# Two heads of a pair by turns in both halves of TensorE's columns, and one exponential and mask for both, in the parallel mixers of a two-block network

## The chip, the core and the metric

The kernel runs on one core of a Trainium2 chip. The metric is the device time of one execution in microseconds; three runs of the kernel before gave 2126.7, 2129.07 and 2130.88 us. The engines are named as in the profile: PE (TensorE, matmuls), DVE (VectorE), ACT (ScalarE), POOL (GpSimd) and SP (which issues the loads).

## The reference

Two different transformer-like blocks follow each other on a sequence of 256 tokens with 1024 features, each of two layers. The change lies in the second block. It puts 16 meta tokens ahead (272 tokens), and each of its layers has a feed-forward part, three mixers side by side and another feed-forward part. The mixers share one input projection and one output projection:

```python
proj = h @ w_in[l]
(z, xbc, dt_raw, fq, fk, fv, f_raw, cq, ckv, k_rope) = jnp.split(proj, IN_SPLITS, axis=-1)
mix = jnp.concatenate([y_ssd, y_fox, y_mla], axis=-1) @ w_out[l]

# fox (4 heads of 64, forget gates c) and mla (4 heads of 96 and 64): causal attention
p = jax.nn.softmax(jnp.where(causal, s, -jnp.inf), axis=-1)
out = jnp.einsum('bhqk,bkhd->bqhd', p, v)

# ssd (8 heads of 64, 2 groups): a state-space mixer, in its quadratic form
seg = jnp.exp(jnp.where(causal, a_cum[..., :, None] - a_cum[..., None, :], -jnp.inf))
cb = jnp.einsum('bclhn,bcshn->bhcls', Cm, Bm)
y_diag = jnp.einsum('bhcls,bcshp->bclhp', cb * seg, xdt)
```

## The kernel before

Features lie on partitions and tokens along the columns. Weight matrices are split in two parts (`wh`, `wl`) on ACT (L100) and DVE (L101), and a projection to 128 features is 24 matmuls over the full array (`pj`, L128 in the mixers, L730 to L732 for the output projection).

`Second.mixer` runs once for each of the two layers. It is a set of generators, each of which yields after a small step: the input projection, `gates`, `latents`, `heads`, `states`, two `attend` for each kind of attention and `ssd`. `run_spread` takes the next step from the generator that is furthest behind its share of the stage. The framework then gives every engine a fixed order of its own, so that PE takes its instructions in that order and one that waits holds back all behind it. Heads go in pairs: with 64 features a head, heads `2c` and `2c + 1` fill the lower and the upper half of the 128 partitions of one PSUM bank (`yp` for attention, `sy` for the decay, one bank each).

In `attend`, a unit is one head `hh` of the pair and one block `i` of queries: `i = 0` the 16 meta tokens (both heads at once), `i = 1` and `i = 2` the blocks of 128. Three steps follow each other, each one turn of the loop behind the other: `score` (PE L558 into `S`, then DVE and ACT: mask, L566 exponential), `turn` (DVE L575, PE transposes L580 into `pt`, copies to `apt` by DVE L581 and ACT L584) and `apply` (PE L597 into `yp`, L592 for `i = 0`). Applying block `i` takes one matmul with the 16 rows of the meta tokens and `i` matmuls with 128 rows, each with 64 stationary columns (the head's `v`) and 128 moving ones.

In `ssd`, each head's cumulated decay is broadcast by two matmuls (L404, L405 into `bc`). For each of the three blocks of keys (`STT`, 128, 128 and 16 rows) DVE subtracts (L661), ACT takes the exponential (L662), DVE multiplies by the masked product `cbm` (L649), and PE multiplies by `xdt` into the head's half of `sy` (L650), with 64 stationary and 272, 144 or 16 moving columns (256 instead of 272 in the last layer, which computes no meta tokens). `held` lets two further blocks start before a block is finished. L669 and what follows it turn `sy` into the output part `yo`.

All these matmuls are float32, which are two records of the trace each; those of the projections (float32r) and the transposes are one record.

Of the kernel before, what the change touches and what calls it, by code (L numbers as in the profile page):

```python
# [10 lines left out]
F32 = mybir.dt.float32  # L11
F32R = mybir.dt.float32r
AF = mybir.ActivationFunctionType
ALU = mybir.AluOpType
ADD, SUB, MUL, MIN, MAX = ALU.add, ALU.subtract, ALU.mult, ALU.min, ALU.max
# [9 lines left out]
STT = [(0, 128), (128, 128), (256, 16)]  # L25
# [276 lines left out]
class Second:  # L302
# [28 lines left out]
    def mixer(self, l, xs, sp, f0):  # L331

        n, nc, P = self.n, self.n.nc, self.n.P
        T, TQ = T2, T2 - f0
        tc = self.n.tc
        with ExitStack() as es:
            es.enter_context(n.psum(pj=2, pt=1, yp=1, bc=1, S=2, sy=1))
            kp = es.enter_context(tc.tile_pool(name="mk", bufs=1))
            tp = es.enter_context(tc.tile_pool(name="mt", bufs=2))
            win = f"w_in{l}"  # L340
            kt = lambda name, w=T, dt=F32: kp.tile([128, w], dt, name=name)
            tt_ = lambda name, w=T, bufs=1: tp.tile([128, w], F32, name=name, bufs=bufs)
            pj = lambda: n.ps("pj", T)
            mm = nc.tensor.matmul
# [9 lines left out]
            toks = kp.tile([128, 3, 72], F32, name="toks")  # L354
# [151 lines left out]
            cbm = []  # L506
# [27 lines left out]
            def attend(c, q, k, v, fox):  # L534

                yp = n.ps("yp", T)
                units = ([] if f0 else [(0, 0)]) + [(hh, i) for i in (1, 2) for hh in range(2)]
                ckbs, tiles, pts = {}, {}, {}

                def score(hh, i):  # L540
                    h = 2 * c + hh
                    q0, qn = FQT[i]
                    kn = q0 + qn
                    if fox and i == 1:
                        ckbs[hh] = tt_("ckb", bufs=2)
                        nc.scalar.copy(ckbs[hh], bcast(32 + h))
                    S = n.ps("S", T)
                    if i == 0:
                        qn = 64
                        for e in range(2):  # L550
                            o = S[32 * e:32 * e + 32, :kn]
                            if fox:
                                j = 32 + h + e
                                mm(o, n.ident[32:64, j:j + 1].to_broadcast([32, 32]), cum[32:64, :kn], start=True, stop=False)
                                mm(o, cum[32:64, 0:32], self.nid[32:64, j:j + 1].to_broadcast([32, kn]), start=False, stop=False)
                            mm(o, q(h + e)[:, 0:32], k(h + e)[:, :kn], start=not fox, stop=True)
                    else:
                        mm(S[:qn, :kn], q(h)[:, q0:q0 + qn], k(h)[:, :kn], start=True, stop=True)  # L558
                    src = S
                    t = tt_("att", bufs=3)  # L560
                    if fox and i:
                        nc.vector.scalar_tensor_tensor(t[:qn, :kn], ckbs[hh][:qn, :kn], tokq[:qn, i, h:h + 1], S[:qn, :kn], op0=SUB, op1=ADD)
                        src = t
                    mn = tp.tile([128, 2], F32, name="amn", bufs=4)
                    nc.vector.tensor_tensor_reduce(t[:qn, :kn], src[:qn, :kn], self.mask[:qn, i, :kn], 1.0, 3.0e38, op0=ADD, op1=MIN, accum_out=mn[:qn, 0:1])
                    nc.scalar.activation(t[:qn, :kn], t[:qn, :kn], AF.Exp, scale=-1.0, bias=mn[:qn, 0:1], accum_out=mn[:qn, 1:2])  # L566
                    tiles[hh, i] = t, mn

                def turn(hh, i):
                    q0, qn = FQT[i]  # L570
                    kn = q0 + qn
                    qn = qn if i else 64
                    t, mn = tiles.pop((hh, i))
                    nc.vector.reciprocal(mn[:qn, 1:2], mn[:qn, 1:2])
                    nc.vector.tensor_scalar(t[:qn, :kn], t[:qn, :kn], mn[:qn, 1:2], None, op0=MUL)  # L575
                    ps = n.ps("pt")
                    pt = pts[hh, i] = tp.tile([128, 3, 128], F32, name="apt", bufs=2)
                    for j in range(i + 1):
                        k0, kk = FQT[j]
                        nc.tensor.transpose(ps[:kk, j * 128:j * 128 + qn], t[:qn, k0:k0 + kk], n.ident[:qn, :qn])  # L580
                    nc.vector.tensor_copy(pt[:16, 0, :qn], ps[:16, :qn])  # L581
                    if i:
                        w = slice(128, 128 + i * 128)
                        nc.scalar.copy(pt[:, 1:1 + i], ps[:, w].rearrange("p (a b) -> p a b", b=128))  # L584

                def apply(hh, i):
                    h = 2 * c + hh
                    q0, qn = FQT[i]
                    pt = pts.pop((hh, i))
                    if i == 0:  # L590
                        for e in range(2):
                            mm(yp[64 * e:64 * e + 64, 0:16], v[:16, 0, 64 * (h + e):64 * (h + e) + 64], pt[:16, 0, 32 * e:32 * e + 16], start=True, stop=True)  # L592
                        return
                    rows = slice(64 * hh, 64 * hh + 64)
                    for j in range(i + 1):
                        kk = FQT[j][1]
                        mm(yp[rows, q0:q0 + qn], v[:kk, j, 64 * h:64 * h + 64], pt[:kk, j, :qn], start=(j == 0), stop=(j == i))  # L597

                for u in range(len(units) + 2):
                    if u < len(units):  # L600
                        score(*units[u])
                    if 0 <= u - 1 < len(units):
                        turn(*units[u - 1])
                    if u >= 2:
                        apply(*units[u - 2])
                    if u == len(units) + 1:
                        key = (4 if fox else 6) + c
                        ys[key] = n.split(kp, f"yo{key}", yp[:, f0:], TQ)
                    yield
# [5 lines left out]
            xdt = kp.tile([128, 3, 512], F32, name="xdt")  # L615
# [16 lines left out]
            def ssd():  # L632
                for i, (s0, sn) in enumerate(STT):
                    ps = n.ps("pt")
                    for c in range(4):
                        nc.tensor.transpose(ps[:sn, ts(c, 128)], xsn[c][:, s0:s0 + sn], n.ident)
                    nc.vector.tensor_tensor(
                        xdt[:sn, i].rearrange("p (h d) -> p h d", h=8),
                        ps[:sn].rearrange("p (h d) -> p h d", h=8),
                        toks[:sn, i, 64:72].rearrange("p (h o) -> p h o", o=1).to_broadcast([sn, 8, 64]), op=MUL)  # L640
                    yield
                held = []

                def finish():
                    yp, h, i, m = held.pop(0)
                    s0, sn = STT[i]
                    e = max(s0, f0)
                    rows = slice(64 * (h % 2), 64 * (h % 2) + 64)
                    nc.vector.tensor_tensor(m[:sn], m[:sn], cbm[h // 4][i][:sn, e - s0:], op=MUL)  # L649
                    mm(yp[rows, e:], xdt[:sn, i, 64 * h:64 * h + 64], m[:sn], start=(i == 0), stop=(i == 2))  # L650

                for c in range(4):
                    yp = n.ps("sy", T)
                    ysum[c] = kt(f"ys{c}")[:, :TQ]
                    for hh in range(2):
                        h = 2 * c + hh
                        bc = bcast(h)
                        for i, (s0, sn) in enumerate(STT):
                            e = max(s0, f0)
                            m = tt_(f"ssm{i}", T - s0, 2)[:, e - s0:]  # L660
                            nc.vector.tensor_scalar(m[:sn], bc[:sn, e:], toks[:sn, i, h:h + 1], 0.0, op0=SUB, op1=MIN)  # L661
                            nc.scalar.activation(m[:sn], m[:sn], AF.Exp)  # L662
                            held.append((yp, h, i, m))
                            if len(held) > 2:
                                finish()
                            yield
                    while held:
                        finish()
                    nc.vector.scalar_tensor_tensor(ysum[c], xsn[c][:, f0:], P(f"dskip{l}", c), yp[:, f0:], op0=MUL, op1=ADD)  # L669
                    if c % 2:  # L670
                        while 16 + c not in have:
                            yield
                        for e in (c - 1, c):
                            nc.vector.tensor_tensor(ysum[e], ysum[e], zs[e], op=MUL)
                        norms(c // 2)
                    yield
# [1254 lines left out]
```

## Time and profile before

| | |
|---|---|
| median of three runs | 2129.07 us |
| the profiled execution | 2128.95 us |
| its span, first to last instruction | 2127.2 us |
| PE busy | 2061.1 us, 97% of the span |
| DVE busy | 1449.9 us, 68% |
| ACT busy | 1099.4 us, 52% |
| mean DMA rate | 159 GB/s |
| first mixer, first to last 64-column matmul | 1240.2 to 1326.9 us |
| second mixer, the same | 1820.2 to 1898.9 us |

A record's duration of a matmul holds its whole way through the array, and matmuls overlap. So a busy share of 100% doesn't tell how fast PE gets on; the distance from one start to the next does. The rows of a timeline merge records of one line that follow each other; their length is then from the first start to the last end.

### The profile page before, as it was taken

The page shows a single profiled execution, that of the slowest core. Times are in us where ns is not written, and L with a number is a line of the kernel's source. Part 1 is how long each engine was busy: PE and PEld are TensorE (multiplying, and loading weights), DVE is VectorE, ACT ScalarE, POOL GpSimd, SP SyncE. Part 2 cuts the span into 40 slices and gives each one's busy share as a digit, 9 for nine tenths or more (in the row PEclk, how much of TensorE's full clock was granted, in tenths as well). Part 3 has the DMA queues.
Part 4 walks back from the last instruction along what each step waited for, and adds up shares of the span by engine and source line. Part 5 has one row for each costly group of instructions (what it writes and reads, how often), then busy time and mean ns, then how long its engine had stood idle before and what let it go on. Part 6 is the DMA issues. An engine that isn't in the chain of part 4 may idle for free.

```text
span 2127.2 us, 43215 instructions
## 1 busy us (share of the span) xinstructions
PE 2061.1 (97%) x17602; PEld 1910.9 (90%) x17602; DVE 1449.9 (68%) x2959; ACT 1099.4 (52%) x2055; POOL 30.3 (1%) x68
## 2 busy tenths in 40 slices
PE   7999999999899989999999999999999999999998
PEld 6888888999888879999999877899999998778998
DVE  7878776886788867556555776755565457767555
ACT  4544446444745555545454744644454537456453
POOL 0000000000011100000000000000000000000000
PEclk9999999999999999999999999999999999999999
DMA  7533323896434237645554321455455543225553
GB/s 269 169 95 124 96 64 117 329 322 213 147 125 145 92 127 260 197 169 184 188 173 167 131 90 60 128 190 171 161 170 182 164 170 128 90 70 178 189 179 119
DMA packets 102087, 337.30 MB, mean 159 GB/s; under 512 B 11456, under 2 KB 19456, under 8 KB 101888
## 3 DMA queue, kind: packets, MB, share of 16 engines
q1 hardware_dynamic: 101888, 334.54, 47.3%
q8 instruction: 138, 2.26, 0.4%
q14 instruction: 61, 0.50, 0.1%
HBM read 333.45 MB, written 1.05 MB: 157 GB/s over the span
## 4 chain that ended last, share of the span: by engine, by line
PE 86%; DVE 7%; ACT 4%; DMA 2%; issue 1%; POOL 1%; SPq 0%; ACTq 0%; DVEq 0%; POOLq 0%
PE pj L157 17%; PE pj L158 17%; PE pj L160 17%; PE pj L128 8%; PE pj L1067 4%; PE B L918 2%; DVE wl L101 2%; PE yp L597 1%; PE pj L148 1%; ACT wh L100 1%; PE G L1170 1%; PE pj L149 1%; PE B L1371 1%; PE sy L650 1%; PE pj L152 1%
## 5 line engine op out<-in xcount | busy, mean ns | idle before, releaser
L101 DVE TENSOR_TENSOR wl<-wr,wh 128x1024 fp32r<-128x1024 f32 (+2 forms) x557 | 641.1, 1160 | 296.5 <-ACT wh L100 142.3
L100 ACT CAST wh<-wr 128x1024 fp32r<-128x1024 f32 (+2 forms) x557 | 555.7, 1002 | 499.1 <-PE pj L158 207.6
L278 DVE TENSOR_TENSOR hh<-sg,pj 128x256 f32<-128x256 f32 (+1 forms) x132 | 56.5, 428 | 148.9 <-PE pj L160 130.0
L829 DVE SCALAR_TENSOR_TENSOR adacc<-adar,cond,adacc 128x512 f32<-128x512 f32 x140 | 104.2, 744 | 10.4 <-DMA adar<-in_ada_dram 8.9
L187 ACT ACTIVATE q<-r 128x256 f32<-128x256 f32 (+1 forms) x80 | 33.3, 422 | 97.4 <-DVE r L208 79.6
L157 PE MATMUL pj<-s0h,wh 128*128 128x256 f32 (+1 forms) x240 | 68.4, 285 | 0.9 <-ACT wh L100 0.9
L160 PE MATMUL pj<-s6h,wl 128*128 128x256 f32 (+1 forms) x240 | 68.6, 286 | 0.0
L158 PE MATMUL pj<-s5l,wh 128*128 128x256 f32 (+1 forms) x240 | 68.4, 285 | 0.0
L157 PE MATMUL pj<-s6h,wh 128*128 128x256 f32 (+1 forms) x240 | 68.4, 285 | 0.0
L158 PE MATMUL pj<-s7l,wh 128*128 128x256 f32 (+1 forms) x240 | 68.3, 285 | 0.0
L160 PE MATMUL pj<-s1h,wl 128*128 128x256 f32 (+1 forms) x240 | 68.3, 284 | 0.0
L160 PE MATMUL pj<-s5h,wl 128*128 128x256 f32 (+1 forms) x240 | 68.2, 284 | 0.0
L160 PE MATMUL pj<-s7h,wl 128*128 128x256 f32 (+1 forms) x240 | 68.2, 284 | 0.0
L160 PE MATMUL pj<-s0h,wl 128*128 128x256 f32 (+1 forms) x240 | 68.2, 284 | 0.0
L160 PE MATMUL pj<-s4h,wl 128*128 128x256 f32 (+1 forms) x240 | 68.2, 284 | 0.0
L157 PE MATMUL pj<-s4h,wh 128*128 128x256 f32 (+1 forms) x240 | 68.2, 284 | 0.0
L158 PE MATMUL pj<-s1l,wh 128*128 128x256 f32 (+1 forms) x240 | 68.1, 284 | 0.0
L160 PE MATMUL pj<-s2h,wl 128*128 128x256 f32 (+1 forms) x240 | 68.1, 284 | 0.0
L158 PE MATMUL pj<-s3l,wh 128*128 128x256 f32 (+1 forms) x240 | 68.0, 284 | 0.0
L157 PE MATMUL pj<-s7h,wh 128*128 128x256 f32 (+1 forms) x240 | 68.0, 284 | 0.0
L157 PE MATMUL pj<-s1h,wh 128*128 128x256 f32 (+1 forms) x240 | 68.0, 283 | 0.0
L157 PE MATMUL pj<-s5h,wh 128*128 128x256 f32 (+1 forms) x240 | 68.0, 283 | 0.0
(1811 smaller groups left out, 7283.2 us busy)
## 6 DMA issues: line engine op xcount, KB each, us to landing
wr<-in_ffn_in_dram SPq DMA_DIRECT2D x264, 512.0 KB, 3.7
wr<-in_ffn_out_dram SPq DMA_DIRECT2D x96, 512.0 KB, 3.5
adar<-in_ada_dram SPq DMA_DIRECT2D x80, 512.0 KB, 4.7
wr<-in_w_in_dram SPq DMA_DIRECT2D x40, 512.0 KB, 3.5
wr<-in_ffn_out_dram SPq DMA_DIRECT2D x48, 384.0 KB, 3.7
wr<-in_gin_dram SPq DMA_DIRECT2D x32, 512.0 KB, 3.7
ada<-in_ada_dram SPq DMA_DIRECT2D x16, 512.0 KB, 7.2
wr<-in_w_out_dram SPq DMA_DIRECT2D x16, 512.0 KB, 3.4
```

Source lines behind the costliest of these rows:

```text
L100: nc.scalar.copy(h, r)
L101: nc.vector.tensor_tensor(l, r, h.bitcast(F32), op=SUB)
L128: mm(o, a, b[:, t0:], start=(c == 0), stop=(c == 23))
L148: mm(o, wh, xs[k][0], start=(i == 0), stop=False)
L157: mm(o, wh, xs[k][0], start=(i == 0), stop=False)
L158: mm(o, wh, xs[k][1], start=False, stop=False)
L160: mm(o, w(k)[1], xs[k][0], start=False, stop=(i == K - 1))
L187: nc.scalar.activation(q[k], d[k], AF.Square)
L278: nc.vector.tensor_tensor(hh, sg, up, op=MUL)
L829: nc.vector.scalar_tensor_tensor(acc, r[:, ts(k, 512)], c, acc, op0=MUL, op1=ADD)
L918: self.anchor = nc.tensor.matmul(out[r, c], lhsT[r, c], rhs[r, c], start=start, stop=start or b == nblk - 1).ins
L1067: nc.tensor.matmul(ps, a, b, start=(k == 0 and i == 0), stop=(k == 7 and i == 2))
```

## The change

In `attend`, `apply` does nothing for the first head of a pair (but for `i = 0`). With the second head it takes both heads' transposed scores, and for each block of keys issues the matmul of head 1 (upper half of the columns) and then that of head 0 (lower half); `issue_after` keeps these two in that order in PE's queue. `apt` has three buffers instead of two.

In `ssd`, the tiles `ssm` hold both heads side by side, as does the mask by a broadcast. The subtraction stays one for each head. The exponential and the mask are one instruction for both heads, after the second head's subtraction, and the two heads' matmuls follow each other. `held` lets one further block start.

```diff
-                    pt = pts[hh, i] = tp.tile([128, 3, 128], F32, name="apt", bufs=2)
+                    pt = pts[hh, i] = tp.tile([128, 3, 128], F32, name="apt", bufs=3)
...
                 def apply(hh, i):
                     h = 2 * c + hh
                     q0, qn = FQT[i]
-                    pt = pts.pop((hh, i))
                     if i == 0:
+                        pt = pts.pop((hh, i))
...
                         return
-                    rows = slice(64 * hh, 64 * hh + 64)
+                    if hh == 0:
+                        return
+                    pair = [pts.pop((e, i)) for e in range(2)]
                     for j in range(i + 1):
                         kk = FQT[j][1]
-                        mm(yp[rows, q0:q0 + qn], v[:kk, j, 64 * h:64 * h + 64], pt[:kk, j, :qn], start=(j == 0), stop=(j == i))
+                        for e in (1, 0):
+                            g = 2 * c + e
+                            with tc.issue_after(at) if e == 0 else nullcontext():
+                                at = mm(yp[64 * e:64 * e + 64, q0:q0 + qn], v[:kk, j, 64 * g:64 * g + 64], pair[e][:kk, j, :qn], start=(j == 0), stop=(j == i)).ins
...
                 def finish():
-                    yp, h, i, m = held.pop(0)
+                    yp, c, i, m = held.pop(0)
                     s0, sn = STT[i]
                     e = max(s0, f0)
-                    rows = slice(64 * (h % 2), 64 * (h % 2) + 64)
-                    nc.vector.tensor_tensor(m[:sn], m[:sn], cbm[h // 4][i][:sn, e - s0:], op=MUL)
-                    mm(yp[rows, e:], xdt[:sn, i, 64 * h:64 * h + 64], m[:sn], start=(i == 0), stop=(i == 2))
+                    w = T - e
+                    pair = m[:, :2 * w].rearrange("p (h t) -> p h t", h=2)
+                    mask = cbm[c // 2][i][:sn, e - s0:].rearrange("p (o t) -> p o t", o=1).to_broadcast([sn, 2, w])
+                    nc.vector.tensor_tensor(pair[:sn], pair[:sn], mask, op=MUL)
+                    for hh in range(2):
+                        h = 2 * c + hh
+                        mm(yp[64 * hh:64 * hh + 64, e:], xdt[:sn, i, 64 * h:64 * h + 64], pair[:sn, hh], start=(i == 0), stop=(i == 2))
...
+                    ms = [tt_(f"ssm{i}", 2 * (T - s0), 2) for i, (s0, sn) in enumerate(STT)]
                     for hh in range(2):
                         h = 2 * c + hh
                         bc = bcast(h)
                         for i, (s0, sn) in enumerate(STT):
                             e = max(s0, f0)
-                            m = tt_(f"ssm{i}", T - s0, 2)[:, e - s0:]
-                            nc.vector.tensor_scalar(m[:sn], bc[:sn, e:], toks[:sn, i, h:h + 1], 0.0, op0=SUB, op1=MIN)
-                            nc.scalar.activation(m[:sn], m[:sn], AF.Exp)
-                            held.append((yp, h, i, m))
-                            if len(held) > 2:
-                                finish()
+                            w = T - e
+                            nc.vector.tensor_scalar(ms[i][:sn, hh * w:hh * w + w], bc[:sn, e:], toks[:sn, i, h:h + 1], 0.0, op0=SUB, op1=MIN)
+                            if hh:
+                                nc.scalar.activation(ms[i][:sn, :2 * w], ms[i][:sn, :2 * w], AF.Exp)
+                                held.append((yp, c, i, ms[i]))
+                                if len(held) > 1:
+                                    finish()
                             yield
```

PE has as many matmuls as before, and SP as many loads; the queues of SP and POOL keep their order, and PE, DVE and ACT differ only from the first mixer's attention to its output projection and in the same part of the second.

PE, the first applies of the first mixer's attention (`mla`), in the kernel before:

```order
L128 MATMUL pj<-s7l,wh 128x272
L128 MATMUL pj<-s7h,wl 128x272
L597 MATMUL yp<-apt,mlaV 64x128
L128 MATMUL pj<-s0h,wh 128x272
L128 MATMUL pj<-s0l,wh 128x272
L597 MATMUL yp<-apt,mlaV 64x128
L128 MATMUL pj<-s0h,wl 128x272
L128 MATMUL pj<-s1h,wh 128x272
```

and the first applies there in the changed kernel (L602 is the apply's new line):

```order
L128 MATMUL pj<-s5h,wh 128x272
L558 MATMUL S<-mlaK,mlaQ 128x144
L602 MATMUL yp<-apt,mlaV 64x128 x2
L128 MATMUL pj<-s5l,wh 128x272
L580 MATMUL pt<-ident,att 16x128
L580 MATMUL pt<-ident,att 128x128 x2
L602 MATMUL yp<-apt,mlaV 64x128 x2
L128 MATMUL pj<-s5h,wl 128x272
```

The first head's two applies, which stood alone between projection matmuls, have moved behind the second head's transposes and stand as pairs.

PE, the decay of the second mixer, heads 4 and 5, in the kernel before (`ssm0`, `ssm1`, `ssm2` are the three blocks of keys):

```order
L128 MATMUL pj_23630<-s2l_22189,wh_23566 128x256
L650 MATMUL sy_23556<-ssm0_23598,xdt_22394 64x256
L404 MATMUL bc_23641<-cumh_22364,identR_13166 128x272
L405 MATMUL bc_23641<-cuml_22365,identR_13166 128x272
...
L128 MATMUL pj_23630<-s4l_22204,wh_23566 128x256
L650 MATMUL sy_23556<-ssm1_23603,xdt_22394 64x144
L128 MATMUL pj_23630<-s4h_22203,wl_23567 128x256
```

and in the changed kernel (L659 is the new line):

```order
L128 MATMUL pj_23567<-s4h_22167,wh_23513 128x256
L659 MATMUL sy_23502<-ssm0_23504,xdt_22358 64x256 x2
L128 MATMUL pj_23567<-s4l_22168,wh_23513 128x256
...
L659 MATMUL sy_23502<-ssm1_23505,xdt_22358 64x144 x2
L128 MATMUL pj_23567<-s6h_22181,wh_23513 128x256
```

One matmul of one head has become two, one for each half, from one tile.

ACT, the decay of the first mixer, heads 4 and 5, in the kernel before:

```order
L662 ACTIVATE ssm0_16936<-ssm0_16936 128x272
L662 ACTIVATE ssm1_16954<-ssm1_16954 128x144
...
L662 ACTIVATE ssm2_16957<-ssm2_16957 16x16
L327 ACT_TABLE_LOAD
L327 ACTIVATE rsy_16918<-pt_16911,c0_79 128x272
L662 ACT_TABLE_LOAD
L662 ACTIVATE ssm0_16973<-ssm0_16973 128x272
L328 ACTIVATE rsy_16918<-rsy_16918 128x272
L662 ACTIVATE ssm1_16978<-ssm1_16978 128x144
```

and in the changed kernel (L673):

```order
L327 ACT_TABLE_LOAD
L327 ACTIVATE rsy_16900<-pt_16893,c0_79 128x272
L673 ACT_TABLE_LOAD
L673 ACTIVATE ssm0_16915<-ssm0_16915 128x544
L328 ACTIVATE rsy_16900<-rsy_16900 128x272
L673 ACTIVATE ssm1_16916<-ssm1_16916 128x288
```

Two exponentials of 272 columns, one on either side of the table loads, have become one of 544 behind them.

## Rows read from the trace of the kernel before

**Rows 1.** The page: the chain that ended last, shares of the span by engine.
```profile
PE 86%; DVE 7%; ACT 4%; DMA 2%; issue 1%; POOL 1%; SPq 0%; ACTq 0%; DVEq 0%; POOLq 0%
```

**Rows 2.** Busy us (instructions) by stretch: PE, PEld, DVE, ACT, POOL; clock, DMA.
```profile
1212.00:1240.00 28.00, 25.69 (x164) 22.15 (x164) 24.07 (x61) 18.59 (x45) 0.20 (x2) 0.94 0.34 109
1240.00:1330.00 90.00, 90.00 (x559) 64.55 (x558) 56.60 (x186) 42.24 (x112) 0.00 (x0) 1.00 0.22 73
...
1820.00:1900.00 80.00, 80.00 (x493) 58.30 (x492) 51.53 (x168) 39.83 (x104) 0.00 (x0) 1.00 0.21 71
```

**Rows 3.** Timeline of PE, first mixer: start, length, line, tiles, shape, records.
```profile
1241.05 0.29 PE L128 MATMUL pj<-s7l,wh 128*128 128x272 f32 x1
1241.18 0.29 PE L128 MATMUL pj<-s7h,wl 128*128 128x272 f32 x1
1241.39 0.43 PE L597 MATMUL yp<-apt,mlaV 16*64 16x128 f32 x2
1241.75 0.39 PE L128 MATMUL pj<-s0h,wh 128*128 128x272 f32 x1
1241.98 0.28 PE L128 MATMUL pj<-s0l,wh 128*128 128x272 f32 x1
1242.19 0.43 PE L597 MATMUL yp<-apt,mlaV 128*64 128x128 f32 x2
1242.56 0.39 PE L128 MATMUL pj<-s0h,wl 128*128 128x272 f32 x1
1242.79 0.29 PE L128 MATMUL pj<-s1h,wh 128*128 128x272 f32 x1
```

**Rows 4.** Timeline of PE: two applies of one head in a row.
```profile
1248.43 0.65 PE L597 MATMUL yp<-apt,mlaV 128*64 128x128 f32 x4
```

**Rows 5.** Timeline of PE: decay matmuls of 272, 144 and 16 columns.
```profile
1313.01 0.29 PE L128 MATMUL pj<-s0l,wh 128*128 128x272 f32 x1
1313.13 0.29 PE L128 MATMUL pj<-s0h,wl 128*128 128x272 f32 x1
1313.35 0.67 PE L650 MATMUL sy<-ssm,xdt 128*64 128x272 f32 x2
1313.95 0.39 PE L128 MATMUL pj<-s1h,wh 128*128 128x272 f32 x1
1314.18 0.29 PE L128 MATMUL pj<-s1l,wh 128*128 128x272 f32 x1
...
1315.91 0.46 PE L650 MATMUL sy<-ssm,xdt 128*64 128x144 f32 x2
...
1316.62 0.28 PE L650 MATMUL sy<-ssm,xdt 16*64 16x16 f32 x2
```

**Rows 6.** Timeline of PE, second mixer: an apply and a decay matmul together.
```profile
1858.32 0.32 PE L597 MATMUL yp<-apt,foxV 128*64 128x128 f32 x1
1858.32 0.34 PE L650 MATMUL sy<-ssm,xdt 128*64 128x144 f32 x1
1858.48 0.27 PE L597 MATMUL yp<-apt,foxV 128*64 128x128 f32 x1
1858.50 0.50 PE L650 MATMUL sy<-ssm,xdt 128*64 128x144 f32 x3
```

**Rows 7.** Timeline of PE: both halves into one bank, elsewhere in the program.
```profile
1276.55 0.29 PE L592 MATMUL yp<-apt,foxV 16*64 16x16 f32 x4
...
73.59 0.86 PE L1170 MATMUL G<-AR,bh 64*64 64x128 f32 x10
```

**Rows 8.** Groups by shape, 1240 to 1330 us: busy, mean ns, idle before.
```profile
L649 DVE TENSOR_TENSOR ssm<-ssm,cb 128x272 f32<-128x272 f32 x7 | 3.0, 426 | 0.4 <-ACT ssm L662 0.4
L649 DVE TENSOR_TENSOR ssm<-ssm,cb 128x144 f32<-128x144 f32 x8 | 2.3, 290 | 0.0
...
L100 ACT CAST wh<-wr 128x1024 fp32r<-128x1024 f32 x10 | 10.4, 1044 | 7.0 <-PE pj L128 7.0
L662 ACT ACTIVATE ssm<-ssm 128x272 f32<-128x272 f32 x7 | 3.0, 426 | 6.6 <-DVE ssm L661 6.6
```

## The prediction

> **What bounds the kernel now.** I read four views: the page's chain of work that ended last, the busy times by stretch, the timeline of TensorE (PE) inside the second block's mixers, and the instruction groups of the two mixers by shape. In the chain, PE's own work is 86% of the span [rows 1]. The change touches only the two mixers of the second block, so the stretch counts, not the span. From 1240 to 1330 us PE shows 90.00 us busy of 90.00, and from 1820 to 1900 us 80.00 of 80.00, while VectorE (DVE) is at 56.60 and 51.53 us, 64% of the 170 us, and ScalarE (ACT) lower still; the granted clock is 1.00 of 2.4 GHz [rows 2]. So PE's rows alone set the pace there: what shortens them shortens the kernel, until DVE or ACT feed PE too late. A busy PE is not a PE at work, though. The starts in the timeline show where its time goes: a projection matmul (`pj`, all 128 columns) follows another after 0.125 us (steps of 0.13 and 0.12 in [rows 3, 5]), but wherever a 64-column matmul (`yp` L597, `sy` L650) stands between two of them, the step is broken.
>
> **What a 64-column run costs.** A float32 matmul is two records here. Take the lone 16-row apply: from the `pj` start at 1241.18 to the second `pj` start behind it, 1241.98, is 0.80 us; two ordinary steps would be 0.25, so it cost 0.55. The 128-row one behind it, 1241.98 to 1242.79, costs 0.56 [rows 3]. Two applies of the same head in a row last 0.65 us instead of 0.43 [rows 3, 4]: one more instruction is 0.22. So of 0.55, 0.22 is the instruction's own and 0.33 is paid once for a run: the wait at its start, its unprefetched first weights, the wait and the weights of the `pj` behind it. The decay matmul of 272 columns costs 1313.13 to 1314.18 less 0.25 = 0.80 [rows 5]. In both cases the price is the row's length plus 0.13 (0.43 to 0.55, 0.67 to 0.80). By that the 144-column one (0.46) costs 0.59 and the 16-column one (0.28) 0.41 [rows 5]. Less 0.33, their own parts are 0.47, 0.26 and 0.08 us; of 256 columns, in the second layer, 0.47 x 256/272 = 0.44.
>
> **Do the two halves run at once?** The pair gains twice: it shares one run, and its two matmuls may overlap, since head 0 writes columns 0 to 63 and head 1 columns 64 to 127. Before never pairs them on purpose, but once they meet: at 1858.32 us an apply on the upper half and a decay matmul on the lower start in the same hundredth, both over 128 rows, and their second records at 1858.48 and 1858.50, 0.16 and 0.18 us later [rows 6]. Alone an apply's second record comes after 0.16 as well (0.43 long, 0.27 of it the second record). Neither slowed the other. These two write different PSUM banks, and the new pairs write one; for that there are the apply of the 16 first tokens, both heads into one bank, four records in 0.29 us where one head's two take 0.28 [rows 5, 7], and the first block's `G`, both halves into one bank with 128 columns, ten recorded passes in 0.86 us, where nine steps of 0.11 and a last record of 0.27 would take some 1.3 [rows 7]. So I take full overlap, at 0.01 us a pair (0.29 against 0.28).
>
> The Trainium skill, "TensorE: Matmul & The Clock Gate", section "Part 3: Packing small matmuls — row/col tiling", speaks against that: weight loads overlap running matmuls only where the row groups differ, and matmuls start in program order. Two heads over the same 128 rows would then go one behind the other; the trace disagrees [rows 6], as the decay matmul's first record stands ahead of the apply's second. By that rule the sum below would lose its second term; it is the second rival.
>
> **The change part by part.**
> - *Fewer runs.* Counted in the order of both programs, the runs of 64-column work fall from 53 to 29 in the first mixer and from 47 to 21 in the second (some decay matmuls already stood in one run before, so fewer vanish than pairs are made). 50 x 0.33 = 16.5 us.
> - *Overlapped halves.* Each mixer has 8 pairs of 16-row applies and 12 of 128-row applies: 40 x 0.22 = 8.8 us over both. Of decays each has four pairs of each of three sizes: 4 x (0.47 + 0.26 + 0.08) + 4 x (0.44 + 0.26 + 0.08) = 3.2 + 3.1 = 6.3. Less 0.01 for each of the 40 + 24 pairs, 0.6. Together 14.5 us.
> - *One exponential and mask.* 24 masks and 24 exponentials vanish. A mask of 272 takes 0.426 us and one of 144 0.290 [rows 8], so 128 columns cost 0.136 and the fixed part is 0.137: 24 x 0.137 = 3.3 us less on DVE. ACT gains no less than nothing (one merged exponential, between 0.426 and twice that). Neither engine is the bound, so I count nothing; it lowers DVE's load below.
> - *Waiting for the second head.* A pair waits for the later head. In PE's order other work stands there: in the second layer, the stretch between a second head's broadcast and its first pair that is the shortest holds sixteen `pj` matmuls, three transposes, a broadcast and a score, over 2 us by the `pj` alone. The third `apt` buffer keeps the first head's transposed scores alive, so no copy waits for an apply of an earlier unit. `issue_after` orders only the two matmuls on PE's own queue and waits for nothing else. Loads (SP) and GpSimd keep their order.
>
> **The sum and the new waits.** 16.5 + 14.5 = 31.0 us of PE rows go. What is late next is DVE with ACT: its 108.1 us less 3.3 must fit in 170 - 31.0 = 139.0 us, 75% instead of 64%. At 64% PE was never idle. At 86% (1212 to 1240 us, 24.07 of 28), PE was idle 2.31 us, 8% [rows 2]. Between them by proportion, (75 - 64)/(86 - 64) x 8.25% = 4.1% of 139.0 = 5.7 us; but that stretch starts the mixer, where little independent work is left to PE, so I take half, 2.9 us, and keep both ends, 0 and 8.25% = 11.5. The profiled execution took 2128.95 us (span 2127.2), within 0.1 of the median of 2129.07. 2128.95 - 31.0 + 2.9 = **2100.8**.
>
> **Rivals.**
> - *Hand-offs bind.* Shorter PE work brings each score and transpose closer to its use, and DVE and ACT go one by one. At the upper end above: 2128.95 - 31.0 + 11.5 = 2109.4. For it: the tightest place, the second layer's last forget-gate pair, leaves, by the steps above, 2.9 us of PE work from a score to its transposes, where the least before is 4.8. Against: PE idles nowhere now, and the shortest stretch of PE work between a unit's transposes and its apply is no shorter than before (0.8 against 0.7 us, by the same steps).
> - *Halves don't overlap* with 128 rows and one bank: only the runs go, 2128.95 - 16.5 = 2112.4. Against it [rows 6, 7].
> - *The gain is given back behind the mixer*, where the output projection waits for `w_out` weights: if half the gain is lost there, 2128.95 - 15.5 = 2113.4. Against: in the first stretch ACT waited 7.0 us for PE to release weight buffers [rows 8], so the loads are paced by PE and come earlier with it.
> - *Slower.* PE takes its work in order, so a pair that isn't ready stops the projections too. If PE stood at each of the 24 decay pairs for the merged exponential and mask (0.85 at most and 0.72, from [rows 8]), 24 x 1.57 = 37.7 us would come back: 2128.95 - 31.0 + 37.7 = 2135.7. It decides from 31.0/24 = 1.3 us of standing at each pair; the 2 us of `pj` in between speak against it.
>
> **How the numbers follow.** Forecast 75%, hand-offs 12%, no overlap 4%, given back 3%, slower 3%, and 3% that such losses add up to no change. The range must leave out no more than 2 in 10: its lower end is no new wait at all, 2097.9, less 1.0 for prices read to 0.02 us over 50 runs and 2.2 for runs that differ (2126.7 to 2130.88): 2094.7. The upper end is the hand-offs' 2109.4 and a little: 2110. A measurement here tells a change from none at about 0.2%, 4.3 us: faster 94%, same 3%, slower 3%.
>
> **What would show it.** Right: applies and decays stand in the timeline as four records in the length of two (about 0.44 and 0.68 us); both mixers are some 14 us shorter; DVE is near 75% in them; PE idles there a few us at most, the rest of the program keeps its times. Wrong: four records in about 0.65 (no overlap), PE idle ahead of `yp` or `sy` rows by over 10 us in all (hand-offs, or the slower case), or a longer wait of the output projection for its weights.

## The result: 28 us less, and where they went

The changed kernel took 2100.3 us (median of 4 runs, 2097.8 to 2102.87) against 2128.57 for the kernel before beside it (2126.7 to 2130.88): a ratio of 0.9858, 95% interval 0.9837 to 0.988. On a second occasion (the first experiment below) the ratio was 0.987 (0.9838 to 0.9902). The forecast was 2100.8. The profiled execution of the changed kernel took 2097.8 us with a span of 2096.0, 31.2 less than the span of before.

The page's chain of work that ended last, the answer to [rows 1], is still led by PE. Its listed shares add up to 77% only, so 66 and 86 can't be set against each other; PE's busy share of the span is 97% on both pages:

```profile
PE 66%; DVE 5%; ACT 3%; DMA 1%; issue 1%; POOL 1%; ACTq 0%; DVEq 0%; POOLq 0%; SPq 0%
```

For the rest I cut each mixer in three: its **start** (from the first broadcast L404 to the first score L558), the **paired stretch** (to the start of the last 64-column record) and its **tail** (to the start of the last matmul of the output projection). Busy times by stretch, columns as in [rows 2], first the kernel before, first mixer and then second:

```profile
1212.67:1228.32 15.65, 13.98 (x88) 12.40 (x87) 12.96 (x29) 12.79 (x30) 0.10 (x1) 0.89 0.40 135
1228.32:1326.90 98.58, 97.94 (x608) 70.79 (x607) 66.11 (x215) 46.95 (x126) 0.00 (x0) 1.00 0.22 71
1326.90:1350.36 23.46, 21.66 (x165) 21.01 (x165) 19.05 (x37) 12.25 (x20) 0.00 (x0) 1.00 0.41 133
1791.12:1808.45 17.33, 15.28 (x84) 13.21 (x83) 12.68 (x28) 12.85 (x30) 0.14 (x2) 0.80 0.40 121
1808.45:1898.90 90.45, 89.90 (x552) 66.16 (x551) 61.42 (x194) 45.24 (x119) 0.00 (x0) 1.00 0.22 71
1898.90:1921.64 22.74, 21.42 (x172) 20.90 (x173) 20.36 (x39) 12.22 (x20) 0.00 (x0) 1.00 0.47 152
```

and the changed kernel, cut at the same events:

```profile
1212.90:1227.40 14.50, 12.85 (x87) 10.98 (x87) 12.68 (x28) 12.26 (x27) 0.10 (x1) 1.00 0.47 146
1227.40:1309.81 82.41, 81.74 (x609) 63.80 (x607) 64.11 (x203) 45.71 (x117) 0.00 (x0) 1.00 0.23 78
1309.81:1333.84 24.03, 21.89 (x167) 21.16 (x167) 20.09 (x38) 12.23 (x20) 0.00 (x0) 1.00 0.47 154
1774.66:1790.61 15.95, 13.89 (x84) 11.81 (x83) 12.36 (x27) 12.33 (x27) 0.13 (x2) 0.89 0.42 131
1790.61:1867.34 76.73, 76.16 (x566) 60.85 (x566) 63.35 (x185) 43.75 (x110) 0.00 (x0) 1.00 0.28 87
1867.34:1890.93 23.59, 20.94 (x159) 20.39 (x160) 18.45 (x37) 11.98 (x20) 0.00 (x0) 0.93 0.45 143
```

Read the first number behind each stretch. The paired stretches fell from 98.58 to 82.41 and from 90.45 to 76.73 us, 29.9 together, at a clock of 1.00 in both kernels. PE's idle time in them (length less PE busy) was 0.64 and 0.55 us and is 0.67 and 0.57: no new wait there, although DVE, with nearly the same busy time in a shorter stretch, went from 67% to 80%. The tails grew by 0.6 and 0.9 us. The starts are 1.15 and 1.38 us shorter, but at a clock of 1.00 and 0.89 against 0.89 and 0.80: they hold the same work, and their length follows the clock, not the change (below). So of the 31.2 us of this one pair of executions some 2.5 are the clock's at the starts, and 31.2 - 2.5 = 28.7 are left. Against that, the second tail of the changed kernel stood at a mean clock of 0.93, which cost it some 1.5 us (worked out below). The medians of the two occasions differ by 28.3 and 30.5 us.

The instructions themselves, timeline of PE, the answer to [rows 3 to 5]:

```profile
1243.31 0.43 PE L602 MATMUL yp<-apt,mlaV 16*64 16x128 f32 x4
1244.33 0.44 PE L602 MATMUL yp<-apt,mlaV 128*64 128x128 f32 x4
...
1248.37 0.66 PE L602 MATMUL yp<-apt,mlaV 128*64 128x128 f32 x8
...
1263.73 0.68 PE L659 MATMUL sy<-ssm,xdt 128*64 128x272 f32 x4
...
1265.36 0.47 PE L659 MATMUL sy<-ssm,xdt 128*64 128x144 f32 x4
...
1267.04 0.29 PE L659 MATMUL sy<-ssm,xdt 16*64 16x16 f32 x4
```

Four records in 0.43 and 0.44 us where one head's two took 0.43; eight in 0.66 where four took 0.65; the decays of both heads in 0.68, 0.47 and 0.29 where one took 0.67, 0.46 and 0.28. The overlap is full in every shape shown.

Where the tails grew, the waits of PE show it. Kernel before, 1318 to 1352 us and then 1870 to 1925:

```profile
PE pj L730 <- DVE r L208: 1.8, 1, 1.8
...
PE pj L730 <- DVE r L208: 1.3, 1, 1.3
```

and the changed kernel, in its first and second mixer:

```profile
PE pj L741 <- DVE r L208: 2.1, 1, 2.1
...
PE pj L741 <- DVE r L208: 2.6, 1, 2.6
```

This is the output projection, ahead of its last two blocks of 128 outputs. They go into the two PSUM banks of `pj`, and these are free only when DVE has read the two blocks before out of them (`r`, L208). The chain of work that ends at this wait, in the second mixer of the changed kernel:

```profile
1875.63 4.80 DMA wr<-in_w_out_dram
...
1882.28 1.14 DVE wl L101
1883.41 0.35 DVE r L208
...
1883.89 0.55 PE pj L741
```

A load of `w_out` takes 4.80 us to land, ACT has stood 1.2 us for it, and DVE comes to `r` only behind a split of weights (`wl`). In the first mixer of both kernels the chain runs through such a load too (4.93 us before, 4.76 after); in the second mixer it did so only after the change. PE stands 0.3 and 1.3 us longer than before: 1.6 us of the gain are given back behind the mixer. (In two more profiles of the same 64-column work, the changed kernel again and the one without turns below, the two waits make 4.6 and 4.5 us; here they make 4.7, before 3.1.)

### The profile page after: what moved, and what is told of

It reads as the page before. It is cut to its first block, busy times and chain, and to the rows that moved or that the text cites. A ratio compares the mean times of both kernels' runs of the same rounds, so it can differ in the third digit from the quotient of the medians.

```text
span 2096.0 us, 43160 instructions
## 1 busy us (share of the span) xinstructions
PE 2028.1 (97%) x17602; PEld 1894.9 (90%) x17602; DVE 1447.1 (69%) x2935; ACT 1094.9 (52%) x2031; POOL 30.3 (1%) x68
## 4 chain that ended last, share of the span: by engine, by line
PE 66%; DVE 5%; ACT 3%; DMA 1%; issue 1%; POOL 1%; ACTq 0%; DVEq 0%; POOLq 0%; SPq 0%
PE pj L157 15%; PE pj L158 15%; PE pj L160 15%; PE pj L128 7%; DVE wl L101 2%; PE pj L148 1%; PE pj L149 1%; PE B L1382 1%; PE pj L152 1%; ACT wh L100 1%; PE yp L602 1%; PE S L558 1%; DVE r L226 1%; DMA wr<-in_w_out_dram 0%; PE pt L580 0%
## 5 line engine op out<-in xcount | busy, mean ns | idle before, releaser
L157 PE MATMUL pj<-s3h,wh 128*128 128x256 f32 (+1 forms) x240 | 68.1, 284 | 0.0
L160 PE MATMUL pj<-s3h,wl 128*128 128x256 f32 (+1 forms) x240 | 68.1, 284 | 0.0
```

Source lines behind the costliest of these rows:

```text
L157: mm(o, wh, xs[k][0], start=(i == 0), stop=False)
L160: mm(o, w(k)[1], xs[k][0], start=False, stop=(i == K - 1))
```

## The experiments

For each kernel the time counts, and from its trace one more number, **S**: paired stretch and tail of both mixers, which leaves the starts and their clock out. S is 235.2 us for the kernel before and 206.8 for the changed one (82.41 + 24.03 + 76.73 + 23.59); in two more executions of the same 64-column work (the changed kernel again and the one without turns, below) it was 206.8 and 206.7.

One thing besides the kernel still moves S. In some tails the granted clock falls to 0.50 for about 3 us behind a wait of PE at the output projection, and the tail's mean is 0.93. The changed kernel's two profiles give the price: its first tail took 24.03 us at 1.00 and 25.33 at 0.93, its second 23.59 at 0.93 and 22.33 at 1.00, with nearly the same waits, so some 1.5 us. Whether the longer waits make such a fall more likely isn't shown. The last column takes 1.5 off for each such tail:

| kernel | S | tails at 0.93 | S at a clock of 1.00 |
|---|---|---|---|
| before | 235.2 | 0 | 235.2 |
| changed (also again, and without turns) | 206.8 | 1 | 205.3 |
| applies alone | 216.7 | 0 | 216.7 |
| decay alone | 225.9 | 1 | 224.4 |
| both heads into one half | 220.2 | 2 | 217.2 |
| own exponential and mask | 207.9 | 0 | 207.9 |
| one more DVE pass | 208.7 | 1 | 207.2 |
| two more DVE passes | 214.1 | 2 | 211.1 |
| two buffers | 207.5 | 1 | 206.0 |
| broadcast over 128 rows | 203.4 | 0 | 203.4 |
| and scores over 128 rows | 201.7 | 2 | 198.7 |

Differences of the last column below 1 us are not read.

**The changed kernel again.** 

> The changed kernel once more, beside its parts on the same chip, so that these are compared with it and not with a run of another day. Every theory expects what was measured before: about 31 us less than the kernel before in the profiled execution (2096.0 us of span against 2127.2), 28 to 31 in the medians.

Measured: 2101.99 us against 2132.46; span 2095.7.

**The applies alone** (the hunks on `apt` and `apply`; `finish` and its loop as before):

```diff
-                        mm(yp[rows, q0:q0 + qn], v[:kk, j, 64 * h:64 * h + 64], pt[:kk, j, :qn], start=(j == 0), stop=(j == i))
+                        for e in (1, 0):
...
+                                at = mm(yp[64 * e:64 * e + 64, q0:q0 + qn], v[:kk, j, 64 * g:64 * g + 64], pair[e][:kk, j, :qn], start=(j == 0), stop=(j == i)).ins
```

> The kernel before with the paired applies (and the third apt buffer) alone; the decay stays one head after the other. By the terms of the prediction: the runs of 64-column work fall from 100 to 70 in the two mixers, 30 x 0.33 = 9.9 us, and 40 overlapped instructions give 40 x 0.22 - 0.4 = 8.4: 18.3 us less. If two halves did not overlap and only the runs counted: 9.9 less. If the gain came from the fewer DVE and ACT instructions of the decay and not from PE's rows: about 0.

Measured: 2112.71 us, ratio 0.9919 (0.989 to 0.9947); S 216.7, 18.5 below before, and PE's waits for `r` are 0.9 us longer (1.9 and 2.1 against 1.8 and 1.3), so 19.4 of PE's rows went. The terms had 18.3; this is far from 9.9 and 0.

**The decay alone** (the hunk on `finish` and its loop; the applies as before):

```diff
-                    mm(yp[rows, e:], xdt[:sn, i, 64 * h:64 * h + 64], m[:sn], start=(i == 0), stop=(i == 2))
+                    for hh in range(2):
+                        h = 2 * c + hh
+                        mm(yp[64 * hh:64 * hh + 64, e:], xdt[:sn, i, 64 * h:64 * h + 64], pair[:sn, hh], start=(i == 0), stop=(i == 2))
```

> The kernel before with the paired decay alone (one exponential and one mask for both heads, then the two matmuls); the applies stay one head after the other. By the terms: the runs fall from 100 to 80, 20 x 0.33 = 6.6 us, and the overlapped decays give 6.3 - 0.2 = 6.1: 12.7 us less, and with the applies alone 18.3 + 12.7 = 31.0, the whole change, with nothing between the two parts. Without overlap: 6.6 less. If DVE's and ACT's instructions were what counts: 3.3 us of DVE, and nothing from the runs.

Measured: 2117.41 us, ratio 0.994 (0.9923 to 0.9957), 15.1 us less by the medians; S 225.9, only 9.4 less. (The profiled execution, 2124.37 us, is the longest of nine. Its first mixer starts 6.4 us later than before's, which S leaves out.) The trace says why S falls short of 12.7. PE's waits in the two tails:

```profile
PE pj L736 <- DVE r L208: 2.7, 1, 2.7
PE pj L736 <- ACT yo2h L79: 0.2, 1, 0.2
...
PE pj L736 <- DVE r L208: 2.1, 1, 2.1
```

are 1.9 us longer than before's 1.8 and 1.3, and the second tail ran at a clock of 0.93, some 1.5 us: 9.4 + 1.9 + 1.5 = 12.8. The two parts by S at a clock of 1.00 give 18.5 + 10.8 = 29.3 of the whole change's 29.9: they add up, with nothing to be told between them.

**Both heads into one half.** The runs stay; the overlap goes in the 128-row applies and in the decays of 144 and 16 columns.

```diff
...
+                                to = e if j == 0 else 1
+                                at = mm(yp[64 * to:64 * to + 64, q0:q0 + qn], v[:kk, j, 64 * g:64 * g + 64], pair[e][:kk, j, :qn], start=(j == 0), stop=(e == 0 and j in (0, i))).ins
...
+                        to = hh if i == 0 else 1
+                        mm(yp[64 * to:64 * to + 64, e:], xdt[:sn, i, 64 * h:64 * h + 64], pair[:sn, hh], start=(i == 0), stop=((i, hh) in ((0, 0), (2, 1))))
```

> The changed kernel in which the second head's matmul (and the first head's) of a pair both write the upper half of the columns in the 128-row applies and in the decays of 144 and 16 columns; the 16-row applies and the decays of 272 and 256 columns stay in two halves. The sums of two heads are mixed by it: what is computed is changed, the instructions and their sizes are not. The count of 64-column runs is the same (50 in the two mixers). If two halves run at once in the changed kernel, 24 x 0.22 + 8 x (0.26 + 0.08) = 8.0 us come back and the four records of a 128-row apply last 0.65 us or more where they lasted 0.43. If halves don't matter and only the count of runs does: no difference to the changed kernel.

Measured: 2113.14 us, ratio 0.9919 (0.9889 to 0.9949), 11.2 us above the changed kernel beside it; S 220.2, 13.4 above, 11.9 at equal clocks. Timeline of PE:

```profile
1250.18 0.65 PE L603 MATMUL yp<-apt,mlaV 128*64 128x128 f32 x4
...
1269.30 1.09 PE L603 MATMUL yp<-apt,mlaV 128*64 128x128 f32 x8
...
1275.40 0.70 PE L661 MATMUL sy<-ssm,xdt 128*64 128x144 f32 x4
...
1278.78 0.40 PE L661 MATMUL sy<-ssm,xdt 16*64 16x16 f32 x4
```

The same instructions, one half for both: 0.65 for 0.44, 1.09 for 0.66, 0.70 for 0.47, 0.40 for 0.29. The steps are 0.21, 0.43, 0.23 and 0.11 us, as the terms had them (0.22, 0.44, 0.26, 0.08). So the overlap is a cause and not a companion. Of the 11.9 us these steps explain 8; another 2.7 are a new wait at the output projection's first round, for the decay's last result (`yo2h`), in the two tails:

```profile
PE pj L743 <- ACT yo2h L79: 2.0, 1, 2.0
...
PE pj L743 <- ACT yo2h L79: 0.7, 1, 0.7
```

The waits for `r` are 0.7 us shorter. The rest, some 2 us, comes with another order of PE's queue and is not split further.

**An exponential and a mask for each head.**

```diff
...
-                    nc.vector.tensor_tensor(pair[:sn], pair[:sn], mask, op=MUL)
+                    for hh in range(2):
+                        nc.vector.tensor_tensor(pair[:sn, hh], pair[:sn, hh], cbm[c // 2][i][:sn, e - s0:], op=MUL)
...
+                            nc.scalar.activation(ms[i][:sn, hh * w:hh * w + w], ms[i][:sn, hh * w:hh * w + w], AF.Exp)
```

> The changed kernel with an exponential and a mask for each head again; the two matmuls of a pair still stand together. It adds 24 masks (24 x 0.137 = 3.3 us of DVE) and 24 exponentials. If PE's rows alone set the pace, as the prediction counted it, no difference to the changed kernel (within 1 us in the stretch from the first score to the last 64-column run, 82.2 and 76.5 us in the two mixers). If the merged exponential and mask were a good part of the gain: 3 us or more come back.

Measured: 2101.58 us, ratio 0.9867 (0.985 to 0.9883); S 207.9, 1.1 more, 2.6 at equal clocks. The time can't tell it from the changed kernel. But, other than expected, the kernel does not undo the merging alone: with a mask for each head, other matmuls come between the two of a pair in 12 of the 24 decay pairs, counted in the order of PE's program. Timeline of PE, one head and then the other:

```profile
1277.98 0.67 PE L659 MATMUL sy<-ssm,xdt 128*64 128x272 f32 x2
...
1279.99 0.67 PE L659 MATMUL sy<-ssm,xdt 128*64 128x272 f32 x2
```

By the terms the overlap of these 12 is worth up to 3.7 us. The 2.6 us and the 1.0 us by which PE's waits for `r` are shorter here (3.7 in place of 4.7) make 3.6 us of PE's rows. So the merging, the third thing that the change does, seems to help by keeping the two matmuls of a pair together; what it is worth beyond that was not isolated.

**More work for DVE in each pair.** One pass more, and two:

```diff
+                    nc.vector.tensor_scalar(pair[:sn], pair[:sn], 1.0, None, op0=MUL)
                     nc.vector.tensor_tensor(pair[:sn], pair[:sn], mask, op=MUL)
```

> The changed kernel with one more DVE pass over every pair of decays ahead of its mask (a multiplication by 1.0): 24 passes of up to 0.72, 0.45 and 0.17 us, by the masks' own rows, 10.7 us of DVE, 80% to 87% of the paired stretch. By the proportion that the prediction used for new waits (8.25% of PE idle at 86%), some 13 us are lost. By the margins that the masks have in the trace of the changed kernel (the shortest 0.34 us in the first mixer, 0.12 in the second, most 0.7 to 1.6) only what exceeds a margin is lost: some 2 us. If hand-offs of the decay never reach PE: 0.

> The same with two more passes, up to 21.3 us of DVE, 94% of the paired stretch: by the proportion some 18 us lost, by the margins some 9 us, and if hand-offs never reach PE, 0. Where PE begins to stand at the decay's weights tells how much room the change left.

Measured: 2102.78 us with one pass (ratio 0.9868, 0.9853 to 0.9882; S 208.7, 1.9 more) and 2111.12 with two (0.9903, 0.9885 to 0.9921; S 214.1, 7.3 more, 5.8 at equal clocks). The passes were lighter than expected: 0.43, 0.30 and 0.16 us by size, not 0.72, 0.45 and 0.17, so DVE came to 81% and 82% of the paired stretches, not 87% and 94%. At those shares the proportion gives some 11 us of idle PE in the stretch; 1.2 and 1.6 were measured, so it is refuted. The margins' 2 and 9 come close, in part by chance, since they were worked out for the heavier passes, and the place is not the one that they named. Paired stretches with two more passes:

```profile
1228.60:1314.17 85.57, 84.87 (x634) 67.19 (x633) 69.26 (x228) 46.02 (x117) 0.00 (x0) 1.00 0.24 81
...
1793.76:1875.56 81.80, 80.95 (x586) 63.87 (x585) 67.56 (x209) 43.44 (x110) 0.00 (x0) 1.00 0.26 85
```

PE idles 0.70 and 0.85 us in them, hardly more than the 0.67 and 0.57 of the changed kernel, with DVE at 81 and 83%. The decays stand later in PE's order among more projection matmuls (634 and 586 instructions where there were 609 and 566), and PE waits behind them:

```profile
PE pj L743 <- ACT yo2h L79: 2.0, 1, 2.0
...
PE pj L743 <- ACT yo2h L79: 2.0, 1, 2.0
...
PE sy L661 <- DVE ssm L658: 0.2, 1, 0.2
```

4.0 of the 7.3 us stand at the output projection's first round, which needs the decay's last result (`yo2h`), 0.2 at a decay pair, and some 1.5 are the clock in a second tail; the rest is not split. With one pass PE's waits for `yo2h` are 1.0 and 0.8 us, all of its 1.9, and none stands at a pair. So the hand-off that runs short first is the mixer's last one.

**Without turns.** In the two-block applies the second head's two matmuls, then the first head's two.

```diff
...
+                    for js in ((0,), range(1, i + 1)):
+                        for e, j in [(e, j) for e in (1, 0) for j in js]:
```

> The changed kernel, but in the applies with two 128-row blocks the second head's two matmuls come first and then the first head's two, in place of turns. If PE overlaps only neighbours in its queue, the eight records last about 0.87 us where they last 0.66 (three instructions of 0.22 in a row in place of two), 8 x 0.22 = 1.8 us in all, which is below what the time can show; the row shows it. If it looks further ahead than one instruction, or if each half has a queue of its own: 0.66 as before.

Measured: 2103.05 us (one run); S 206.7. Timeline of PE:

```profile
1255.04 0.66 PE L603 MATMUL yp<-apt,mlaV 128*64 128x128 f32 x8
```

Still 0.66, where one behind the other took 1.09. The turns are not needed: a matmul for the free half starts although the second of two for the other half, ahead of it in the queue, has not started.

**Two buffers for the transposed scores** (`bufs=2` again).

> The changed kernel with two buffers for the transposed scores as before, in place of three. The pair holds both, so the copies of the next unit wait for the pair's applies on PE, and DVE and ACT with them. If the prediction is right that the third buffer is what keeps that wait away: some of 12 units wait, for up to the 1 to 2 us that lie between a copy and its apply in the trace, and 2 to 10 us come back. If the copies have room anyway: 0.

Measured: 2103.53 us, ratio 0.9878 (0.9857 to 0.9898); S 207.5, 0.7 more. No difference that can be told; the third buffer isn't what keeps a wait away.

**Fewer tile changes by another way.** The broadcast over 128 rows, and then the forget-gate scores too:

```diff
-            cumh = kp.tile([64, T], F32R, name="cumh")
+            cumh = kp.tile([128, T], F32R, name="cumh")
...
-                sel = self.identR[0:64, row:row + 1].to_broadcast([64, 128])
+                sel = self.identR[:, row:row + 1].to_broadcast([128, 128])
...
+                        nc.scalar.mul(fq[2 * c + e][r, f0:], o[r], -0.125)
```

(The last line is of the second kernel alone.)

> The changed kernel with the decay's broadcast over all 128 rows (the sums carried in 128 partitions in place of 64, the selecting column over 128 rows): the same result, one tile size fewer. A broadcast of 64 rows between two projection matmuls now takes 0.89 us from the start of the one ahead to the start of the second behind it, where four ordinary steps of 0.125 would take 0.50. If the break in the run, and not the 64 columns, is what costs, 24 x 0.39 = 9.4 us go, with no column pairing at all. If only 64-column tiles pay, or if the waits behind the mixer take it back: 0.

> The kernel with the broadcast over 128 rows, and besides the forget-gate scores over 128 rows (the queries of each head in a tile of its own with zeros in the other head's rows). 16 scores of 64 rows stand in the two mixers, each between matmuls of 128 rows or beside another 64-row instruction; if each run costs about 0.33 us like those of 64 columns, up to 16 x 0.33 = 5.3 us more go than with the broadcast alone. Against it: eight more instructions on ACT for the queries, and scores that now run beside a broadcast on the other 64 rows lose that. If row halves that meet save as much as the runs cost: 0 beside the broadcast alone.

Measured: 2098.15 us (ratio 0.9852, 0.9834 to 0.987) and 2095.14 (0.9839, 0.9823 to 0.9854). S is 203.4 and 201.7, 3.4 and 5.1 below the changed kernel, 1.9 and 6.6 at equal clocks. For the broadcast the direction is right and the size, at equal clocks, a fifth of the 9.4 that was expected. For the scores beside it the size is nearly the expected 5.3 as well: 4.7 at equal clocks, and the two paired stretches together fell from 157.6 to 152.8 us. Timeline of PE with the broadcast over 128 rows:

```profile
1281.66 0.29 PE L128 MATMUL pj<-s2l,wh 128*128 128x272 f32 x1
1281.79 0.29 PE L404 MATMUL bc<-cumh,identR 128*128 128x272 f32 x1
1281.91 0.29 PE L405 MATMUL bc<-cuml,identR 128*128 128x272 f32 x1
1282.13 0.51 PE L558 MATMUL S<-fk,fq 64*128 64x144 f32 x2
```

The broadcast now keeps the step of 0.125, but where a 64-row score follows it the break only moves behind it: in the order of PE's program, from the first broadcast to the last 64-column matmul of each mixer, the changes of tile size fall by 24 (272 to 248), not by two for each of 24 broadcasts. The estimate took all of them for lone ones. And here a decay pair does wait:

```profile
PE sy L659 <- DVE ssm L656: 0.4, 1, 0.4
...
PE sy L659 <- DVE ssm L656: 0.7, 1, 0.7
```

1.1 us that the changed kernel didn't have (with the scores too, 0.4). With both, the paired stretches are 78.95 and 73.86 us where the changed kernel's are 82.41 and 76.73; its time is the lowest measured, 5 to 7 us under the changed kernel's two medians, though the intervals of the ratios overlap a little.

## Why the prediction was right, and where it was not

- *What bounds.* Right. PE's rows set the pace before and after: in the paired stretches PE idles 1.2 us of 189.0 before and 1.2 of 159.1 after.
- *Fewer runs and overlapped halves, 16.5 + 14.5 = 31.0.* Right in sum, and near it apart. S fell by 28.4 us; with the 1.6 us of longer waits at the output projection and some 1.5 for the clock of 0.93 in the second tail, 31.5 of PE's rows went. By the same account the applies alone are 19.4 for 18.3 and the decays alone 12.8 for 12.7; the overlap taken away by itself brought back its 8 and some 2 more. The price of a run was not taken apart by itself. The kernel with both heads in one half, which keeps the fewer runs, lies 18.0 us under the kernel before in S at equal clocks, with 3.6 us of longer waits: 21.6 for the terms' 31.0 - 8.0 = 23.0. What stands behind the sum is that every price was read from lone and joined rows of the same shapes [rows 3 to 5], and that the overlap had been seen twice before it was made [rows 6, 7].
- *The overlap rival* fell: four records last as long as two. The rule in the Trainium skill ("TensorE: Matmul & The Clock Gate", section "Part 3: Packing small matmuls — row/col tiling") that matmuls start strictly in order doesn't hold here: without turns the first head's matmuls stand behind two of the second head's, and all eight records still last 0.66 us, where 1.09 is measured for one behind the other.
- *One exponential and mask, counted at nothing.* Right in the time, where nothing can be told. In S 2.6 us come back at equal clocks without it, most likely because half of the decay pairs then fall apart: the prediction counted on the pairs without saying that the merged mask helps to hold them together.
- *New waits, +2.9.* This term was wrong in its place and in its rule. It put the waits inside the mixer, by a proportion between DVE's share and PE's idle time. DVE rose by 13 points (67% to 80%) where 11 were forecast (64% to 75%), and PE's idle time there did not move (1.19 us before, 1.24 after; the proportion gives 9.5 at 80%, its half 4.8). 1.6 us turned up in the tail instead. That the median came within 0.5 us of the forecast is in part luck: with 1.6 in place of 2.9 the sum is 2099.6, and the clock moves single executions by more than these differences.
- *Hand-offs bind.* Not here, but near: two more DVE passes in each pair cost 7 to 11 us, and with 128-row broadcasts decay pairs begin to wait.
- *Given back behind the mixer* named the right place and the right load at ten times its size: PE's wait for `r` hangs on a load of `w_out`, and 1.6 us were given back, not 15.5. The argument that the loads come earlier with PE did not hold in the second mixer, where the load stands in the chain only after the change.
- *Slower* would have needed 1.3 us of standing at each pair; none is seen at a pair in the waits of the changed kernel. (The sixteen `pj` that spoke against it are 1.9 us at the second layer's step of 0.12, not over 2.)
- *The third buffer* was credited with keeping copies from waiting. With two no difference can be told: that sentence had no row behind it.

## What to carry to other kernels

Where a busy engine sets the pace, price what breaks its step: a lone 64-column matmul cost 0.55 us where its own part is 0.22, so by the terms putting equals side by side was worth more than half of this gain, before any overlap. When work is taken off such an engine, look for the new wait not only inside the stretch but behind it: here it was a PSUM bank that DVE freed late, behind a load of weights, and with more work on DVE the mixer's last result. And a share of busy time foretells no wait: DVE went from 67% to 80% of the paired stretches, and PE's idle time in them stayed.

## What the runs showed of the hardware

- *Halves go by themselves.* Two matmuls over the same 128 rows, on columns 0 to 63 and 64 to 127, run at once in every shape tried, into one PSUM bank, and with two of one half ahead of the other in the queue (0.66 us for eight records either way).
- *Row halves do too.* In the changed kernel a broadcast over rows 0 to 63 and a score over rows 64 to 127 met, both on 128 columns, each with its usual length:

```profile
1282.79 0.39 PE L404 MATMUL bc<-cumh,identR 64*128 64x272 f32 x1
1282.80 0.39 PE L558 MATMUL S<-fk,fq 64*128 64x144 f32 x1
1283.02 0.28 PE L405 MATMUL bc<-cuml,identR 64*128 64x272 f32 x1
1283.03 0.28 PE L558 MATMUL S<-fk,fq 64*128 64x144 f32 x1
```

  Scores of two heads could be paired in this way; it wasn't tried.
- *The clock at the mixers' starts is not the same in every execution.* The changed kernel's second profile:

```profile
1212.50:1229.58 17.08, 15.43 (x88) 13.49 (x87) 12.70 (x28) 12.15 (x27) 0.10 (x1) 0.80 0.38 124
1776.62:1791.37 14.75, 12.71 (x83) 10.71 (x82) 12.30 (x27) 12.32 (x27) 0.12 (x2) 1.00 0.44 142
```

  The first start took 14.50 us in the other profile, at 1.00, and the second 15.95, at 0.89. In all 13 profiles of this study, whichever the kernel, a first start took about 14.5, 15.6 or 17.1 us and a second 14.8, 15.9 or 17.3. In the kernel with the decay alone the granted clock goes from 1.00 (2.4 GHz) to 0.50 (1.2 GHz) after PE was busy for only 0.46 and 0.35 of a us in two rows:

```profile
1220.00:1221.00 1.00, 0.46 (x2) 0.29 (x2) 0.49 (x3) 0.99 (x2) 0.00 (x0) 1.00 0.84 344
1221.00:1222.00 1.00, 0.35 (x2) 0.29 (x2) 0.79 (x3) 0.99 (x4) 0.00 (x0) 0.71 0.58 164
1222.00:1223.00 1.00, 1.00 (x3) 0.29 (x2) 0.48 (x2) 0.98 (x4) 0.00 (x0) 0.50 0.83 315
```

  Both starts together can so differ by up to 5 us between two executions (1.4 in the changed kernel's two profiles, 30.45 and 31.83), as much as its runs scatter (2097.8 to 2102.87). Ahead of the first mixer, where all these kernels are alike, the first broadcast came between 1211.9 and 1219.0 us. So a difference of two profiled spans is worth little below that.
